# RG-LRU gates as 64x64 quadrants of the array, and an earlier split of w_ukv

## The chip, the cores and the metric

One core of a Trainium2 chip runs one launch of a whole transformer layer. The metric is the device time of that launch in microseconds (us); lower is better. TensorE (PE) multiplies, VectorE (DVE), ScalarE (ACT) and GpSimd (POOL) do the elementwise work, and SyncE (SP) issues all DMAs, in order. All data are float32 in memory; matmuls take either f32 operands or operands that were split into a high and a low part (fp32r).

## What is computed

A layer on 1024 latent and 256 context tokens (1280 columns together). The part that matters here is the RG-LRU mixer, 512 channels wide, and what follows it:

```
xr, gr, cq, ckv, kr = split(h @ w_in)             # gr, cq for latent tokens
xc = depthwise_conv(xr)                           # 4 taps
for d in (forward, backward):
    r = sigmoid(xc_by_head @ w_a[d] + b_a[d])     # 8 heads of 64 channels
    i = sigmoid(xc_by_head @ w_x[d] + b_x[d])
    log_a = -8 * r * softplus(-lam[d])
    h[d] = scan(a = exp(log_a), u = sqrt(-expm1(2*log_a)) * i * xc)   # context first, then latents
y_lru = (h[0] + h[1]) * gelu(gr)
keys, values = rms_norm(ckv) @ w_ukv ; queries = rms_norm(cq) @ w_uq  # MLA, 8 heads
x = x + gate1 * norm([y_lru, attention] @ w_out) ; x = x + gate2 * norm(conv_ffn(x))
```

The gates `r` and `i` multiply each head's 64 channels by a 64x64 matrix of that head.

## The kernel before

Channels lie on partitions, tokens on columns. The stage of the change is the loop over eight 128-channel blocks `m` of `w_in`: blocks 0 to 3 are `xr`, 4 to 7 `gr`. For each, `proj` makes the projection pf (L492, L494, L496: high and low parts, 128x512 pieces) in a PSUM buffer of 1536 columns; there are two such buffers (tag "big"), which projections and gates share. Between the projections `mod2_step` multiplies pages of `w_mod` for later stages (L424: 128x32 strips of the array, four 32-row outputs; L433 and L436 turn the result).

For m = 0 to 3, `conv` copies the projection (L532, L533 on ACT) and makes the convolution `xc[m]` on DVE (L537). The gates of block m come one projection later (`after = {1:0, 2:1, 3:2, 5:3}`): `gate` (L543) multiplies `xc[m]`, 128 channels, by a 128x128 block `wg` that holds two heads on its diagonal and zeros elsewhere, in three column pieces (`CH3`: 512, 512, 256), and ACT takes the sigmoid (L545). A block has four gates (two directions, r and i). `coefs` (L565, L566 on ACT; L567 on DVE) and `scans` follow: the square roots (L573 on ACT), then on DVE L578, L579, and two scans for each direction (L581, L582; L585, L587) and their sum (L591). `gated` multiplies the sum by the gelu of pf4 to pf7 (L552 on ACT, L553 on DVE).

For m = 5 the gates of block 3 run, then `tok_norm`, `ckv_t` (transposes L637, L641 and L642), then `scans(3)`. For m = 6 `w_ukv` is loaded and split by `prep_w` into `wkh` (L69 on ACT) and `wkl` (L76 on DVE). After the loop the cq transposes (L699, evacuated by L701 on ACT and L702 on DVE), five `values` blocks (L713 to L715, six matmuls each) and the keys (L728) follow, in four PSUM buffers; the cq transposes use two of them, so the third and fourth values wait for the two L702. POOL splits `w_uq` (L73, L76).

In this stage the order on each engine is made by the framework's scheduler when the program is built; engines then run in order and wait by semaphores. Pages of 128x1280 come from a pool R of 12, of 128x1024 from a pool L of 30 and W of 5; a load waits until its page is free.

Of the kernel before, what the change touches and what calls it, by code (L numbers as in the profile page):

```python
# [7 lines left out]
F32 = mybir.dt.float32  # L8
# [26 lines left out]
def hybrid_layer_kernel(ctx: ExitStack, tc: tile.TileContext, A, out):  # L35
    nc = tc.nc
    V, S, G, T = nc.vector, nc.scalar, nc.gpsimd, nc.tensor
# [10 lines left out]
    def L(dt=F32, shape=(128, 1024)):  # L48
        cnt[0] += 1
        return lp.tile(list(shape), dt, tag="L", name=f"l{cnt[0]}")  # L50

    def W(dt=F32, shape=(128, 1024)):
        cnt[0] += 1
        return wp.tile(list(shape), dt, tag="W", name=f"w{cnt[0]}")

    def R(dt=F32, shape=(128, 1280)):
        cnt[0] += 1
        return rp.tile(list(shape), dt, tag="R", name=f"r{cnt[0]}")
# [19 lines left out]
    def split(src, hi, lo_, eh, el):  # L78
        copy(eh, hi, src)
        return lo(el, lo_, src, hi)  # L80
# [10 lines left out]
    def P(name, i=0, n=None):  # L91
        o, w = _OFF[name]
        n = w - i if n is None else n
        return pk[:, o + i:o + i + n]
# [254 lines left out]
    for n in range(4, 16):  # L349
        b, kp = order[n]  # L350
# [122 lines left out]
    CH3 = ((0, 512), (512, 512), (1024, 256))  # L473

    def load_w(src):
        t = W()
        nc.sync.dma_start(out=t, in_=src)
        return t

    def prep_w(raw, eh, el):  # L480
        hi, lw = W(F32R), W(F32R)
        split(raw, hi, lw, eh, el)
        return hi, lw

    def proj(w, chunks, name):

        hi, lw = w
        po = ps1.tile([128, 1536], F32, tag="big", name=name, bufs=2)
        for k in range(8):
            wh, wl = hi[:, k * 128:(k + 1) * 128], lw[:, k * 128:(k + 1) * 128]  # L490
            for t0, n in chunks:
                T.matmul(po[:, t0:t0 + n], wh, h_rng(hhi, k, t0, n), start=(k == 0), stop=False)  # L492
            for t0, n in chunks:
                T.matmul(po[:, t0:t0 + n], wh, h_rng(hlo, k, t0, n), start=False, stop=False)  # L494
            for t0, n in chunks:
                T.matmul(po[:, t0:t0 + n], wl, h_rng(hhi, k, t0, n), start=False, stop=(k == 7))  # L496
        return po
# [20 lines left out]
    wg = {}  # L518

    def load_wg(m):  # L520
        wg[m] = L(F32, (128, 4, 128))
        nc.sync.dma_start(out=wg[m], in_=A["wg"][:, m * 512:(m + 1) * 512].rearrange("p (i n) -> p i n", i=4))

    SEG = ((0, SEQ), (SEQ, CTX))
    xc = {}

    def conv(m, po):

        xr = R()
        x = xc[m] = R()  # L530
        cw = [P("cw", m * 4 + k, 1) for k in range(4)]
        S.activation(xr, po[:, 0:NTOK], AF.Copy)  # L532
        S.activation(x, po[:, 0:NTOK], AF.Identity, scale=cw[2], bias=P("cb", m, 1))  # L533
        for o, n in SEG:
            for k, d in ((0, -2), (1, -1), (3, 1)):
                a, b = (o - d, o + n) if d < 0 else (o, o + n - d)
                V.scalar_tensor_tensor(out=x[:, a:b], in0=xr[:, a + d:b + d], scalar=cw[k], in1=x[:, a:b],  # L537
                                       op0=ALU.mult, op1=ALU.add)

    def gate(m, d, g):  # L540
        po = ps1.tile([128, 1536], F32, tag="big", name=f"pg{m}{d}{g}", bufs=2)
        for a, n in CH3:
            T.matmul(po[:, a:a + n], wg[m][:, d * 2 + g, :], xc[m][:, a:a + n], start=True, stop=True)  # L543
        r = R()
        S.activation(r, po[:, 0:NTOK], AF.Sigmoid, bias=P("bx" if g else "ba", d * 4 + m, 1))  # L545
        return r
# [3 lines left out]
    def gated(m, po):  # L550
        g = R()
        S.activation(g[:, :SEQ], po[:, :SEQ], AF.Gelu_apprx_tanh)  # L552
        V.tensor_tensor(ysum[m], ysum[m], g[:, :SEQ], ALU.mult)  # L553
# [4 lines left out]
    def coefs(m, ri):  # L558

        au = []  # L560
        for d in range(2):
            r, i = ri[d]
            c = slice(d * 4 + m, d * 4 + m + 1)
            a = R()
            S.activation(a, r, AF.Exp, scale=n8[:, c])  # L565
            S.activation(r, r, AF.Tanh, scale=p4[:, c])  # L566
            V.tensor_tensor(i, i, xc[m], ALU.mult)  # L567
            au.append((a, r, i))
        return au

    def scans(m, au):
        for a, b, h in au:
            S.activation(b, b, AF.Sqrt)  # L573
        hs = []
        for d in range(2):
            a, b, h = au[d]

            V.scalar_tensor_tensor(out=b, in0=a, scalar=1.0, in1=b, op0=ALU.add, op1=ALU.mult)  # L578
            V.tensor_tensor(h, b, h, ALU.mult)  # L579
            if d == 0:  # L580
                V.tensor_tensor_scan(out=h[:, SEQ:], data0=a[:, SEQ:], data1=h[:, SEQ:], initial=0.0, op0=ALU.mult, op1=ALU.add)  # L581
                V.tensor_tensor_scan(out=h[:, :SEQ], data0=a[:, :SEQ], data1=h[:, :SEQ], initial=h[:, NTOK - 1:NTOK],  # L582
                                     op0=ALU.mult, op1=ALU.add)
            else:
                V.tensor_tensor_scan(out=h[:, SEQ:][:, ::-1], data0=a[:, SEQ:][:, ::-1], data1=h[:, SEQ:][:, ::-1],  # L585
                                     initial=0.0, op0=ALU.mult, op1=ALU.add)
                V.tensor_tensor_scan(out=h[:, :SEQ][:, ::-1], data0=a[:, :SEQ][:, ::-1], data1=h[:, :SEQ][:, ::-1],  # L587
                                     initial=h[:, SEQ:SEQ + 1], op0=ALU.mult, op1=ALU.add)
            hs.append(h)
        ysum[m] = L()  # L590
        V.tensor_tensor(ysum[m], hs[0][:, :SEQ], hs[1][:, :SEQ], ALU.add)  # L591
# [60 lines left out]
    after = {1: 0, 2: 1, 3: 2, 5: 3}  # L652
# [5 lines left out]
    for n, m in enumerate(order):  # L658
        po = proj(ws, CH3 if m < 4 else CH3[:2], f"pf{m}")
        if n < 7:  # L660
            ws = prep_w(raw, "a", "v")
            if n < 6:
                raw = load_w(A["w_fm"][order[n + 2]])
        for s_ in STEPS2[n]:
            mod2_step(s_)
        if m < 4:
            load_wg(m)
            conv(m, po)
        else:
            gated(m - 4, po)  # L670
        if m in after:
            au = coefs(after[m], gates(after[m]))
            if m == 5:
                tok_norm()
                ckv_t()
            scans(after[m], au)
        if m == 6:
            raw = load_w(A["w_ukv"])
            wkh, wkl = prep_w(raw, "a", "v")
    pe_ctx.close()  # L680
    pe_ctx = ExitStack()
    ps2 = pe_ctx.enter_context(tc.tile_pool(name="ps2", bufs=4, space=PSUM, reuse_waits="tile"))
# [438 lines left out]
    for i in range(8):  # L1121
        po = out_tile(i)
# [296 lines left out]
    with tc.manual_schedule():  # L1419
# [13 lines left out]
        o, st = up_steps(*raw, V)  # L1433
# [47 lines left out]
        for j in range(1, NP):  # L1481
            if j + 1 < NP:
                if j == 1:
                    o, st = o2, {n: st2[n] for n in ("sums", "hi_u", "lo_u", "hi_g", "lo_g")}
                else:
                    o, st = up_steps(*raw)
# [7 lines left out]
            else:  # L1494

                o, nxt = None, None
# [258 lines left out]
```

## Time and profile before

| | |
|---|---|
| runs | 1312.43, 1312.20, 1311.76 us, median 1312.2 |
| profiled execution | 1312.39 us |
| its span, first to last instruction | 1310.6 us |
| mean granted PE clock | 0.99 |
| PE busy | 1272.8 us (97%) |
| DVE, ACT, POOL busy | 1011.1, 733.7, 387.3 us |
| gate matmuls (L543) | 96 instructions, 123.1 to 229.1 us |
| first attention matmul | 290.2 us |

The projection and gate stage is from about 90 to 253 us of the span. "Busy" PE means that a matmul is in it, not that all of the array works. The chain of waits goes back from the last instruction through whatever released each step; a row of the timeline merges equal instructions that follow each other and names, in brackets, how long the engine stood before them and what ended that.

### The profile page before, as it was taken

The page shows a single profiled execution, that of the slowest core. Times are in us where ns is not written, and L with a number is a line of the kernel's source. Part 1 is how long each engine was busy: PE and PEld are TensorE (multiplying, and loading weights), DVE is VectorE, ACT ScalarE, POOL GpSimd, SP SyncE. Part 2 cuts the span into 40 slices and gives each one's busy share as a digit, 9 for nine tenths or more (in the row PEclk, how much of TensorE's full clock was granted, in tenths as well). Part 3 has the DMA queues.
Part 4 walks back from the last instruction along what each step waited for, and adds up shares of the span by engine and source line. Part 5 has one row for each costly group of instructions (what it writes and reads, how often), then busy time and mean ns, then how long its engine had stood idle before and what let it go on. Part 6 is the DMA issues. An engine that isn't in the chain of part 4 may idle for free.

```text
span 1310.6 us, 17934 instructions
## 1 busy us (share of the span) xinstructions
PE 1272.8 (97%) x6490; PEld 1050.5 (80%) x6490; DVE 1011.1 (77%) x1665; ACT 733.7 (56%) x1374; POOL 387.3 (30%) x366
## 2 busy tenths in 40 slices
PE   5999999899999999999998999999999999999997
PEld 2796666687999999888877888888888888888886
DVE  3653577767898888856579898778777878897798
ACT  3543675557999999954365334433443344434581
POOL 2410000224666666743100433343244330000013
PEclk8999999999999999999999999999999999999999
DMA  9533234000000000242322222221222149205043
GB/s 372 198 123 125 93 121 145 25 1 2 2 1 2 2 1 17 96 163 97 144 85 91 100 71 90 97 86 65 92 97 81 65 143 354 97 1 177 2 145 128
DMA packets 41320, 124.21 MB, mean 95 GB/s; under 512 B 4600, under 2 KB 4880, under 8 KB 41232
## 3 DMA queue, kind: packets, MB, share of 16 engines
q1 hardware_dynamic: 41232, 123.07, 26.4%
q8 instruction: 51, 0.84, 0.3%
q14 instruction: 37, 0.30, 0.1%
HBM read 101.02 MB, written 22.03 MB: 94 GB/s over the span
## 4 chain that ended last, share of the span: by engine, by line
PE 83%; DVE 10%; ACT 4%; issue 2%; DMA 1%; SPq 0%; POOL 0%; DVEq 0%; ACTq 0%; POOLq 0%
PE b L1217 10%; PE b L1216 10%; PE b L1215 10%; PE t L914 5%; PE po L1063 4%; PE b L1391 4%; PE b L1393 4%; PE b L1392 4%; PE pg L543 3%; PE s L878 3%; PE o L938 3%; PE o L939 3%; PE s L879 3%; PE s L880 2%; DVE l L76 2%; PE po L1066 2%
## 5 line engine op out<-in xcount | busy, mean ns | idle before, releaser
L1217 PE MATMUL b<-l,f 128*128 128x512 f32 x620 | 242.7, 392 | 2.2 <-DVE f L76 2.2
L1215 PE MATMUL b<-l,f 128*128 128x512 f32 x620 | 242.7, 391 | 1.9 <-ACT f L1190 1.4
L1216 PE MATMUL b<-l,f 128*128 128x512 f32 x620 | 242.5, 391 | 0.9 <-DVE l L76 0.9
L1217 PEld LDWEIGHTS b<-l,f 128*128 128x128 f32 x620 | 117.1, 189 | 27.2 <-DVE f L76 3.0
L1215 PEld LDWEIGHTS b<-l,f 128*128 128x128 f32 x620 | 117.1, 189 | 27.0 <-ACT f L1190 1.9
L1216 PEld LDWEIGHTS b<-l,f 128*128 128x128 f32 x620 | 117.1, 189 | 26.1 <-DVE l L76 1.7
L1190 ACT ACTIVATE f<-w 128x1024 fp32r<-128x1024 f32 x21 | 22.3, 1060 | 202.0 <-POOL w L1187 193.7
L906 POOL TENSOR_SCALAR r<-r,c 128x512 f32<-128x512 f32 (+1 forms) x128 | 101.4, 805 | 97.7 <-DVE c L901 68.6
L883 DVE TENSOR_REDUCE c<-s 128x1 f32<-128x512 f32 (+1 forms) x192 | 108.7, 594 | 26.0 <-PE s L880 24.5
L76 DVE TENSOR_TENSOR f<-w,f 128x1024 fp32r<-128x1024 f32 (+1 forms) x90 | 98.3, 1094 | 33.9 <-ACT f L1190 32.9
L1274 DVE SCALAR_TENSOR_TENSOR l<-f,c,l 128x1023 f32<-128x1023 f32 x88 | 121.2, 1378 | 0.7
L894 ACT ACTIVATE r<-s,c 128x512 f32<-128x512 f32 (+1 forms) x192 | 117.7, 621 | 6.2 <-DVE c L901 4.7
L1184 POOL TENSOR_TENSOR w<-w 128x512 f32<-128x512 f32 x19 | 24.5, 1289 | 301.3 <-DVE f L76 301.3
L76 DVE TENSOR_TENSOR l<-t,l 128x512 fp32r<-128x512 f32 x128 | 81.5, 678 | 1.5 <-ACT l L69 1.3
L914 PE MATMUL t<-c,r 128*128 128x128 f32 x640 | 81.7, 273 | 0.9 <-DVE r L76 0.6
L69 ACT ACTIVATE l<-t 128x512 fp32r<-128x512 f32 x128 | 69.5, 595 | 8.6 <-PE t L914 7.8
L914 PEld LDWEIGHTS t<-c,r 128*128 128x128 f32 x640 | 71.3, 140 | 2.6 <-PE t L914 0.8
L1268 ACT ACTIVATE l<-f,c 128x1024 f32<-128x1024 f32 x44 | 54.5, 1238 | 31.7 <-DVE f L1255 31.2
L1614 POOL TENSOR_TENSOR f<-f,w 128x1024 f32<-128x1024 f32 (+1 forms) x5 | 11.8, 2372 | 202.7 <-ACT l L1580 202.7
L878 PE MATMUL s<-r,w 96*128 96x512 f32 (+1 forms) x192 | 69.5, 362 | 1.0 <-ACT r L894 0.7
L1063 PE MATMUL po<-l,r 128*128 128x512 f32 x256 | 69.3, 390 | 0.0
L938 PE MATMUL o<-l,r 128*128 128x256 f32 x256 | 69.0, 303 | 0.0
(355 smaller groups left out, 3195.3 us busy)
## 6 DMA issues: line engine op xcount, KB each, us to landing
w<-in_w_up SPq DMA_DIRECT2D x44, 512.0 KB
r<-in_w_mod SPq DMA_DIRECT2D x32, 512.0 KB
act<-l SPq DMA_DIRECT2D x22, 512.0 KB
l<-in_w_m SPq DMA_DIRECT2D x16, 512.0 KB
l<-act SPq DMA_DIRECT2D x27, 256.0 KB
l<-in_w_dn SPq DMA_DIRECT2D x27, 256.0 KB
w<-in_w_fm SPq DMA_DIRECT2D x8, 512.0 KB
w<-in_w_out SPq DMA_DIRECT2D x8, 512.0 KB
```

What stands on the lines that cost most here:

```text
L76: return (V if e == "v" else G).tensor_tensor(o, src, f(hi), ALU.subtract)
L878: T.matmul(ps[:, :n], qh[0:96, q], kh[0:96, a:a + n], start=True, stop=False)
L883: V.tensor_reduce(out=stat[:, i % 4, c:c + 1], in_=sc[i, c][:, :CK[c][1]], op=ALU.min, axis=AX.X)
L894: S.activation(pt_[i][:, a:a + n], sc.pop((i, c))[:, :n], AF.Exp, scale=-1.0, bias=st[:, 3:4], accum_out=st[:, 4 + c:5 + c])
L906: G.tensor_scalar(out=p[:, a:a + n], in0=p[:, a:a + n], scalar1=stat[:, i % 4, 7:8], scalar2=1.0, op0=ALU.mult, op1=ALU.mult)
L914: T.transpose(ps[:, c, :], pt_[i][:, (c0 + c) * 128:(c0 + c + 1) * 128], ident)
L938: T.matmul(OT[j], v, hi, start=(c == 0), stop=False)
L1063: T.matmul(po[:, n * 512:(n + 1) * 512], w, wo[k][0][:, n * 512:(n + 1) * 512], start=st, stop=en)
L1215: T.matmul(po, wh, bh, start=k == 0 and b == wb[0][1], stop=False)
L1216: T.matmul(po, wh, bl, start=False, stop=False)
L1217: T.matmul(po, wl, bh, start=False, stop=k == 3 and b == wb[-1][1])
L1274: V.scalar_tensor_tensor(out=x[:, a], in0=x0[:, b], scalar=P("fcw", j * 3 + k, 1), in1=x[:, a], op0=ALU.mult, op1=ALU.add)
```

## The change

The gates no longer use one 128x128 block. `load_wg` stores the two 64x64 matrices of each gate twice: `wg[m][:, 0]` as they are, and `wg[m][:, 1]` with the two halves of the partitions swapped, in four DMAs of 64x4x64 instead of one of 128x512. `conv` makes a copy `xcs[m]` of `xc[m]` with its two halves of partitions swapped, by two DMAs of 64x1280 from SBUF to SBUF. `gate` multiplies columns 512 to 1023 on the off-diagonal quadrants of the array (rows 64-127 to output 0-63 and rows 0-63 to output 64-127, from the swapped copies), and columns 0 to 511 and 1024 to 1279 on the diagonal quadrants. What follows the first matmul of a block's first gate in the program is kept behind it by `issue_after`. In the loop, `scans(3)` moves from m = 5 to m = 6, behind the split of `w_ukv`.

```diff
     def load_wg(m):
-        wg[m] = L(F32, (128, 4, 128))
-        nc.sync.dma_start(out=wg[m], in_=A["wg"][:, m * 512:(m + 1) * 512].rearrange("p (i n) -> p i n", i=4))
+
+        wg[m] = L(F32, (128, 2, 4, 64))
+        src = A["wg"][:, m * 512:(m + 1) * 512].rearrange("p (i n) -> p i n", i=4)
+        for x in range(2):
+            for b in (0, 64):
+                p = b ^ (64 * x)
+                nc.sync.dma_start(out=wg[m][p:p + 64, x], in_=src[b:b + 64, :, b:b + 64])
...
+        y = xcs[m] = R()
+        for p in (0, 64):
+            nc.sync.dma_start(out=y[64 - p:128 - p, :], in_=x[p:p + 64, :])
+
     def gate(m, d, g):
+
         po = ps1.tile([128, 1536], F32, tag="big", name=f"pg{m}{d}{g}", bufs=2)
-        for a, n in CH3:
-            T.matmul(po[:, a:a + n], wg[m][:, d * 2 + g, :], xc[m][:, a:a + n], start=True, stop=True)
+        first = None
+        for pieces in (((1, 512, 512), (0, 0, 512)), ((0, 1024, 256),)):
+            for x, a, n in pieces:
+                for o in (0, 64):
+                    h = o ^ (64 * x)
+                    i = T.matmul(po[o:o + 64, a:a + n], wg[m][h:h + 64, x, d * 2 + g, :], (xcs if x else xc)[m][h:h + 64, a:a + n],
+                                 start=True, stop=True, tile_position=(h, o))
+                    if first is None and (d, g) == (0, 0):
+                        first = i
+                        ctx_q.enter_context(tc.issue_after(first.ins))
+        ctx_q.close()
...
             if m == 5:
                 tok_norm()
                 ckv_t()
-            scans(after[m], au)
+                au3 = au
+            else:
+                scans(after[m], au)
         if m == 6:
             raw = load_w(A["w_ukv"])
             wkh, wkl = prep_w(raw, "a", "v")
+            scans(3, au3)
```

The order of the built programs shows it at three places. PE, the first gate of the first group (pm is the modulation, pg the gate), before:

```order
L424 MATMUL pm_952<-r_966,c_77 32x512 x2
L543 MATMUL pg_1109<-r_976,l_973 128x512
L433 MATMUL pm_1074<-c_84,r_1072 128x2 x4
L424 MATMUL pm_1084<-r_1064,c_77 32x512 x2
L424 MATMUL pm_1084<-r_1065,c_77 32x512 x2
L543 MATMUL pg_1109<-r_976,l_973 128x512
L543 MATMUL pg_1109<-r_976,l_973 128x256
```

And after, where the gate is line 558 (r_988 is the swapped copy, r_979 the convolution itself):

```order
L424 MATMUL pm_952<-r_966,c_77 32x512 x2
L558 MATMUL pg_1121<-r_988,l_973 64x512
L433 MATMUL pm_1080<-c_84,r_1078 128x2 x4
L424 MATMUL pm_1090<-r_1070,c_77 32x512 x2
L424 MATMUL pm_1090<-r_1071,c_77 32x512 x2
L558 MATMUL pg_1121<-r_988,l_973 64x512
L558 MATMUL pg_1121<-r_979,l_973 64x512 x2
L558 MATMUL pg_1121<-r_979,l_973 64x256 x2
```

One off-diagonal matmul stands alone ahead of L433, the other five together behind the modulation; the later gates have their six in a row. In the third group three L424 matmuls that stood behind the next projection now stand between the second and the third gate.

ACT, from the last square roots to the first cq evacuation, before (r_1657 is direction 0, r_1669 direction 1, w_1828 the high half of `w_ukv`, pf_1770 the projection pf6):

```order
L573 ACT_TABLE_LOAD
L573 ACTIVATE r_1657<-r_1657 128x1280
L573 ACTIVATE r_1669<-r_1669 128x1280
L552 ACT_TABLE_LOAD
L552 ACTIVATE r_1823<-pf_1770 128x1024
L69 ACTIVATE w_1828<-w_1826 128x1024
L552 ACTIVATE r_1881<-pf_1832 128x1024
```

After, with lines 593 for 573 and 572 for 552:

```order
L593 ACT_TABLE_LOAD
L593 ACTIVATE r_1720<-r_1720 128x1280
L69 ACTIVATE w_1888<-w_1886 128x1024
L572 ACT_TABLE_LOAD
L572 ACTIVATE r_1883<-pf_1830 128x1024
L593 ACT_TABLE_LOAD
L593 ACTIVATE r_1738<-r_1738 128x1280
L572 ACT_TABLE_LOAD
L572 ACTIVATE r_1953<-pf_1904 128x1024
```

The high half of `w_ukv` and the gelu of pf6 moved between the roots of the two directions, with two more table loads.

DVE at the same place, before (w_1829 is the low half of `w_ukv`):

```order
L578 SCALAR_TENSOR_TENSOR r_1657<-r_1677,r_1657 128x1280
L578 SCALAR_TENSOR_TENSOR r_1669<-r_1681,r_1669 128x1280
L579 TENSOR_TENSOR r_1663<-r_1657,r_1663 128x1280
L579 TENSOR_TENSOR r_1675<-r_1669,r_1675 128x1280
L581 SCALAR_TENSOR_TENSOR r_1663<-r_1677,r_1663 128x256
L585 SCALAR_TENSOR_TENSOR r_1675<-r_1681,r_1675 128x256
L582 SCALAR_TENSOR_TENSOR r_1663<-r_1677,r_1663 128x1024
L587 SCALAR_TENSOR_TENSOR r_1675<-r_1681,r_1675 128x1024
L553 TENSOR_TENSOR l_1492<-l_1492,r_1823 128x1024
L591 TENSOR_TENSOR l_1768<-r_1663,r_1675 128x1024
L76 TENSOR_TENSOR w_1829<-w_1826,w_1828 128x1024
L553 TENSOR_TENSOR l_1768<-l_1768,r_1881 128x1024
```

After (598 for 578, 599 for 579, 573 for 553, 601, 602, 605, 607 for the scans, 611 for the sum):

```order
L598 SCALAR_TENSOR_TENSOR r_1720<-r_1749,r_1720 128x1280
L76 TENSOR_TENSOR w_1889<-w_1886,w_1888 128x1024
L599 TENSOR_TENSOR r_1729<-r_1720,r_1729 128x1280
L573 TENSOR_TENSOR l_1552<-l_1552,r_1883 128x1024
L601 SCALAR_TENSOR_TENSOR r_1729<-r_1749,r_1729 128x256
L602 SCALAR_TENSOR_TENSOR r_1729<-r_1749,r_1729 128x1024
L598 SCALAR_TENSOR_TENSOR r_1738<-r_1753,r_1738 128x1280
L599 TENSOR_TENSOR r_1747<-r_1738,r_1747 128x1280
L605 SCALAR_TENSOR_TENSOR r_1747<-r_1753,r_1747 128x256
L607 SCALAR_TENSOR_TENSOR r_1747<-r_1753,r_1747 128x1024
L611 TENSOR_TENSOR l_1902<-r_1729,r_1747 128x1024
L573 TENSOR_TENSOR l_1902<-l_1902,r_1953 128x1024
```

The low half of `w_ukv` moved from the tenth place behind the first L578 to right behind it, and direction 0 now goes through its scans before direction 1 begins.

## Rows read from the trace of the kernel before

**Rows 1.** The page: PE's part 1, and part 4 by engine.
```profile
PE 1272.8 (97%) x6490; PEld 1050.5 (80%) x6490; DVE 1011.1 (77%) x1665; ACT 733.7 (56%) x1374; POOL 387.3 (30%) x366
PE 83%; DVE 10%; ACT 4%; issue 2%; DMA 1%; SPq 0%; POOL 0%; DVEq 0%; ACTq 0%; POOLq 0%
```

**Rows 2.** PE in order of time (start, length), modulation and first gate group.
```profile
105.10 2.78 PE L424 MATMUL pm<-r,c 128*32 128x512 f32 x24
...
123.08 1.12 PE L543 MATMUL pg<-r,l 128*128 128x512 f32 x2
124.04 0.95 PE L433 MATMUL pm<-c,r 128*128 128x2 f32 x8
...
131.58 1.06 PE L424 MATMUL pm<-r,c 128*32 128x512 f32 x6
132.57 4.56 PE L543 MATMUL pg<-r,l 128*128 128x512 f32 x12
136.79 0.93 PE L492 MATMUL pf<-l,w 128*128 128x512 f32 x3
```

**Rows 3.** PE in order of time, the modulation behind pf4.
```profile
203.20 2.59 PE L424 MATMUL pm<-r,c 128*32 128x512 f32 x14
```

**Rows 4.** ACT in order of time, the last gate group.
```profile
220.21 1.06 ACT L69 ACTIVATE w<-w 128x1024 fp32r<-128x1024 f32 x1
221.29 1.28 ACT L545 ACT_TABLE_LOAD   x1
222.58 1.33 ACT L545 ACTIVATE r<-pg,c 128x1280 f32<-128x1280 f32 x1
...
225.65 0.68 ACT L641 ACTIVATE l<-ck,c 128x512 fp32r<-128x512 f32 x1
...
229.16 1.33 ACT L545 ACTIVATE r<-pg,c 128x1280 f32<-128x1280 f32 x1 [0.82 <-PE pg L543]
```

**Rows 5.** The chain that ended last (start, length, what), 218 to 300 us.
```profile
239.18 1.28 ACT r L573
...
240.48 2.90 DVE r L578 x2
243.38 5.10 DVE r L579 x2
...
262.58 0.43 PE pb L715
...
266.33 0.23 PE pb L715
```

**Rows 6.** DVE and POOL in order of time, scans and w_uq.
```profile
205.60 2.88 DVE L579 TENSOR_TENSOR r<-r,r 128x1280 f32<-128x1280 f32 x2
...
260.23 2.46 DVE L702 SCALAR_TENSOR_TENSOR l<-pb,c,l 128x1024 fp32r<-128x1024 f32 x2
...
242.87 2.22 POOL L76 TENSOR_TENSOR l<-l,l 128x768 fp32r<-128x768 f32 x1 [9.61 <-PE pf L494]
```

**Rows 7.** PE in order of time, cq transposes, values and keys.
```profile
251.40 1.91 PE L699 MATMUL pb<-c,l 128*128 128x128 f32 x16
...
259.23 0.80 PE L714 MATMUL pb<-w,l 128*128 128x512 f32 x1 [5.68 <-DVE w L76]
...
268.44 0.39 PE L728 MATMUL pb<-l,w 128*128 128x512 f32 x1
```

**Rows 8.** Two stretches: each engine's busy us (count), then granted clock, DMA.
```profile
180.00:230.00 50.00, 50.00 (x204) 29.54 (x197) 41.21 (x53) 32.17 (x28) 0.00 (x0) 1.00 0.35 111
230.00:262.00 32.00, 26.32 (x120) 21.69 (x119) 24.16 (x17) 17.85 (x17) 6.98 (x4) 0.93 0.09 25
```

**Rows 9.** DVE, SP and POOL in order of time: first convolution, loads of w_uq.
```profile
108.16 4.86 DVE L537 SCALAR_TENSOR_TENSOR r<-r,c,r 128x1022 f32<-128x1022 f32 x6 [1.21 <-ACT r L533]
...
229.17 14.16 SPq L691 DMA_DIRECT2D l<-in_w_uq  x2
...
232.43 0.84 POOL L73 TENSOR_SCALAR l<-l 128x768 fp32r<-128x768 f32 x1 [59.97 <-DMA l<-in_w_uq]
```

More of the change, by code (lines that the diff above doesn't have):

```diff
@@ L520, in load_wg @@
     def load_wg(m):
-        wg[m] = L(F32, (128, 4, 128))
-        nc.sync.dma_start(out=wg[m], in_=A["wg"][:, m * 512:(m + 1) * 512].rearrange("p (i n) -> p i n", i=4))
+        wg[m] = L(F32, (128, 2, 4, 64))
[4 more added lines that the diff above has]
+                nc.sync.dma_start(out=wg[m][p:p + 64, x], in_=src[b:b + 64, :, b:b + 64])
     SEG = ((0, SEQ), (SEQ, CTX))
-    xc = {}
+    xc, xcs = {}, {}
+    ctx_q = ExitStack()
     def conv(m, po):
```

## The prediction

> **What bounds the kernel now.** I read the page first: PE is busy for 97% of the span and carries 83% of the chain that ended last, DVE 10% [rows 1]. Time is therefore won where PE does less, or where it stands. Then I read PE in order of time where the change works. In the gate groups PE goes from projection to gates to projection without standing: in the first group, 123.08 to 136.79 us, 12 gate instructions (two gates of 1280 columns; every f32 matmul is two instructions) take from 132.57 to 136.79, so 2.11 us a gate [rows 2]. From 229 us on it is another matter. The chain leaves PE with the last sigmoid and runs through ACT (Exp, Tanh, Sqrt) to DVE's scan chain, which starts at 240.48 [rows 4, 5]; PE meanwhile does two projections and the cq transposes, begins the values, and stands 5.68 us from 253.55 until DVE has made the low half of `w_ukv` [rows 7]. When it starts again its clock is at half: the same matmul takes 0.43 us at 262.58 and 0.23 at 266.33, and the mean granted clock of 230 to 262 is 0.93 [rows 5, 8]. From the keys (268.44) PE runs on into attention [rows 7], so what the keys gain, the end gains. The profiled execution took 1312.39 us (span 1310.6), the median of the three runs is 1312.2; I count against 1312.4.
>
> **A gate.** Now it is 512+512+256 columns of a 128x128 block with half of its entries zero. After: six 64x64 matmuls, two of 512 columns on the off-diagonal quadrants, two of 512 and two of 256 on the diagonal. The product of 512 columns costs 2.11x512/1280 = 0.84 us by itself, 256 cost 0.42. What the trace of before does not show is 64 rows of the array working beside the other 64. Bounds: one after another a gate would take 4x0.84+2x0.42 = 4.2 us; all four at once, the fullest quadrant has 768 columns, 0.6x2.11 = 1.27 us. The nearest row is the modulation (L424), 32-column strips of the array with different data: 24 instructions, three times four matmuls of 512 columns, take 2.78 us from 105.10 [rows 2], 2.72 of them ahead of the next projection; one by one they would take 12x0.84 = 10.1 us, so four do run at once, at 0.91 us a four. It has 128 rows and four strips, not two by two, but it is four independent f32 matmuls at once, which is the question; so I take 0.91x768/512 = 1.36 us a gate and gain 0.75.
>
> **The groups.** In every group the first off-diagonal matmul of the first gate stands alone, ahead of L433 or L436 (the order of PE), so that gate is 0.84+1.36 = 2.20 and loses 0.09. Three gates gain 2.25. The gates now change the array's shape against the 128x128 work around them, about two changes more a group; a lone gate matmul takes 0.96 from 123.08 to 124.04 where a run gives 0.84 [rows 2], so 0.12 a change, 0.2 a group. Net 1.95 a group, 5.9 for m = 0, 1, 2. PSUM has two buffers for gates, so gate n+2 waits for sigmoid n (1.33 us [rows 4]); with L424 work between the gates this does not bind there. For m = 2 the 14 L424 instructions of 203.20 (2.59 us) [rows 3] become 6 between the gates (1.06 like the six at 131.58 [rows 2]) and 8 where the 14 were (one and the same four, so as much): 0.5 gained. PE reaches the last group 6.4 us earlier.
>
> There ACT binds: the first sigmoid starts right behind its table load (221.29, 222.58 [rows 4]), which moves with PE's group, to 216.2. Now the four sigmoids wait for PE and end at 229.16+1.33 = 230.5. After, a gate (1.36) costs no more than a sigmoid, and they run back to back with the 0.66 us of L641 (225.65 [rows 4]) between: 4x1.33+0.66 = 6.0, end 222.2. **The scan chain starts 8.3 us earlier**, since from the last sigmoid to its start the same instructions follow (240.48 becomes 232.2).
>
> **The scan chain and the values.** Ahead of DVE's first L702 (the low half of cq, which frees the PSUM buffer of the third values block) the order shows the same twelve instructions in both programs: L76 only moves from behind the scans to between them. Their time also contains a collision: L579 takes 5.10 us for two where two took 2.88 at 205.60, while POOL splits `w_uq` (242.87) [rows 5, 6]. POOL is released by the eighth matmul of the last projection, which moves with everything else, so I leave that as it is; were it gone, 5.10-2.88 = 2.2 us would come back. So the first L702 ends 8.3 earlier, at 261.4-8.3 = 253.1 [rows 6].
> On ACT the split of `w_ukv` moves between the two L573 and costs two more table loads: d = 1 gets its root 4.7 us later (L69 1.06, L552 about as much, two loads of 1.28 [rows 4]). That hides as long as DVE is still in direction 0: ahead of that need it has one L578 and one L579 (half of 2.90 and of 5.10 [rows 5], 4.0 us) and L76, L553 and two scans besides. L69 and L552, and behind them DVE's L553, wait for the projection pf6; it starts behind the last gates and moves with them, as the scan chain does.
> PE: the last two projections end at 251.4 now [rows 7]; they move by the group's 6.4 and by what ACT leaves of the gates' gain in the last group, 1.2, to 243.8. Transposes take 1.9, two values of six matmuls (0.23 each at full clock [rows 5]) 2.7: 248.4. They no longer wait for L76. The third does wait, for L702 at 253.1: **4.7 us of standing, in place of 5.68**. Then three values are left, 4.1 us, at full clock. Now keys start (268.44) 7.0 us behind the first L702. If the clock stays up they start 4.1 behind it: 2.9 more. If it falls as before, the half pace costs 2.5 us (259.23 to 264.7) and only 0.4 remains. 4.7 is nearer to 5.68 than to nothing; I take the fall. **Gain 8.3+0.4 = 8.7 us; 1312.4-8.7 = 1303.7.** With the clock up 1301.2; with that and gates of 1.27 us 1300.3.
>
> **What else is issued.** Per m, two DMAs of 64x1280 (640 KB) that swap the halves of `xc`, and four for `wg` instead of one. They go into SP's queue, where the swap waits for the convolution and holds the `w_mod` and `w_fm` loads behind it. A load lands about 3.3 us after its issue (229.17 to 232.43) [rows 9]. The first convolution ends at 113.0 [rows 9], its gates start at 123.08, so 10 us cover twice that size; the other groups have more. Loads behind it are issued 6 us later than now, but are needed 10 or more later. The tightest is one `w_mod` page of m = 1, issued as the modulation ahead of the group starts and multiplied about 4.4 us later: 0 to 1 us. All this costs nothing while that cover holds. The new R pages take slots of the same 12; one wait is new, L532 of m = 2 behind L433, about 1 us on ACT, covered by PE's L424.
>
> **Rivals.**
> *The halves of a bank exclude each other (slower).* Both diagonal matmuls write PSUM columns 0-511, both others 512-1023: one bank, two halves of the partitions, from different halves of the rows. If such writes are taken in turn, only one diagonal and one off-diagonal matmul run together: 2x0.84+2x0.42 = 2.53 a gate, 0.42 over now, and the first gates 0.84+2.53 = 3.37, 1.26 over: 12x0.42+4x1.26 = 10.1, and 0.8 for the changes of shape, less 0.9 (the modulation and the values), so 1322.4; with nothing at all at once 16x2.1 more than now, about 1345. It decides from about 2.15 us a gate. Against it: L424's four strips write one bank at once; but they share their rows, these do not.
> The Trainium skill, "TensorEngine Tiling (Array Packing)", section "Gotcha 1: PSUM Pressure", says that different row tiles cannot access the same PSUM bank at the same time; by that rule the kernel lands on this rival. No run here shows it yet.
> *Only two at a time.* If halves of the columns run together but halves of the rows take turns, a gate is 2x0.84+0.42 = 2.1, as now; PE is where it was and only the values move: 0.4 to 2.9 less 0.8 for the changes of shape, 1310.3 to 1312.8. For it: no row shows row halves; against: nothing in L424 hints that rows matter.
> *A late load or DVE.* Quadrants work, but a late `w_mod` page, or DVE (41 of 50 us busy before 230 [rows 8]) reaching the R pages late, stops PE or the sigmoids for 1 to 2 us in two or three groups: gain 3 to 6, 1306 to 1309.5. For it: several sigmoids now start within 0.5 us of the scan that frees their page.
>
> **Numbers.** Forecast (1299.5 to 1305.5, with the two clocks and the bounds of a gate) 0.70; late load 0.10; two at a time 0.12; banks or nothing at once 0.08. The first two hold 0.8, so the range is 1299.5 to 1309.5. A measurement tells 0.2%, 2.6 us. Faster by more: 0.70+0.10+0.01 = 0.81; within: 0.11; slower: 0.08.
>
> **What would show it.** Two gates in a row in 2.7 us and not 4.2; next projections starting 2, 4 and 6 us earlier; the last four sigmoids back to back; L578 near 232; PE waiting for L702, no longer for L76; half clock there or not. It is wrong if a gate takes 2.1 us or more, if PE waits for the swapped copies, or if DVE waits in direction 1 for ACT's late root.

## The result and the profile after

| | before | after |
|---|---|---|
| runs, median | 1312.32 us (1311.76 to 1313.38, 4 runs) | 1305.22 us (1304.05 to 1307.54, 4 runs) |
| ratio, 95% interval | | 0.9947 (0.9930 to 0.9964) |
| profiled execution, its span | 1312.39, 1310.6 | 1307.54, 1305.7 |
| PE busy | 1272.8 us | 1265.6 us |
| last sigmoid starts | 229.16 [rows 4] | 223.56, the second of the two in the row from 222.33 |
| DVE's last scans start | 240.48 [rows 5] | 234.88 |
| PE stands ahead of the values | 5.68 [rows 7] | 5.66 |
| keys start | 268.44 [rows 7] | 264.05 |
| first attention matmul | 290.19 | 285.76 |

7.1 us were gained where 8.7 were forecast. The profiled execution of after happens to be the slowest of the four, with 4.9 us of gain, and 4.4 of these are there at the first attention matmul. The traces start their clocks at different points: the 24 instructions of L424 ahead of all gates begin at 105.10 in before [rows 2] and at 104.32 in after. So I compare the *stage* from there to the first attention matmul: 185.1 us before, 181.4 in this execution. From the first attention matmul on, every trace of this study takes 1018.8 to 1020.4 us, so what the stage gains, the end gains, to within 1.6 us. The four longest of these tails (1020.0 us and more, in before, after, rows_ahead and evac) go with the lowest granted clock near 710 us (0.83 or 0.84 over 20 us there, 1.00 in after_again), a place that no kernel of this study changes: of the 3.6 us between the profiled executions of after and after_again, about 1 lies there.

PE in order of time, first gate group (start, length, count):

```profile
122.30 1.07 PE L558 MATMUL pg<-r,l 64*64 64x512 f32 x2
123.30 1.05 PE L433 MATMUL pm<-c,r 128*128 128x2 f32 x8
...
125.27 1.51 PE L558 MATMUL pg<-r,l 64*64 64x512 f32 x10
126.72 1.90 PE L424 MATMUL pm<-r,c 128*32 128x512 f32 x10
128.55 1.52 PE L558 MATMUL pg<-r,l 64*64 64x512 f32 x12
...
130.99 2.81 PE L558 MATMUL pg<-r,l 64*64 64x512 f32 x24
133.94 0.85 PE L492 MATMUL pf<-l,w 128*128 128x512 f32 x3
```

Two gates (24 instructions) take 2.81 us where two took 4.56 [rows 2], so four quadrants do run at once. The group from its first gate matmul to the next projection is 11.64 us, 13.71 before: 2.07 gained, and in the second group 2.05 (10.79 for 12.84).

The gain does not arrive whole. PE in order of time at the modulation behind pf4, which answers to [rows 3]:

```profile
197.02 1.05 PE L424 MATMUL pm<-r,c 128*32 128x512 f32 x4
199.87 1.05 PE L424 MATMUL pm<-r,c 128*32 128x512 f32 x4 [1.80 <-DMA r<-in_w_mod]
200.85 0.80 PE L492 MATMUL pf<-l,w 128*128 128x512 f32 x2
...
202.30 1.05 PE L496 MATMUL pf<-l,w 128*128 128x512 f32 x2
...
205.30 0.62 PE L492 MATMUL pf<-l,w 128*128 128x512 f32 x2
```

PE waits 1.80 us for a page of `w_mod`, and then works at half clock (a granted clock of 0.5): a row of two projection matmuls takes 1.05 where it takes 0.62 three microseconds later. The last group starts at 215.42, 3.3 us before its old time (218.68), or 2.5 with the traces laid on each other, that is less the 0.78 us between their two starts of L424, and not 6.4. What held the page, in the chain of waits (start, length, what):

```profile
190.36 0.42 DVE r L444
190.80 3.63 DMA gt<-r
194.51 5.31 DMA r<-in_w_mod
```

SP's waits from 170 to 210 us (total, times, longest), and SP in order of time:

```profile
...
SPq L445 <- DVE r L444: 6.6, 1, 6.6
...
SPq L548 <- DVE r L543: 2.3, 1, 2.3
...
SPq L411 <- DMA gt<-r: 1.6, 1, 1.6
```

```profile
185.79 0.23 SPq L445 DMA_DIRECT2D gt<-r  x1
...
189.52 1.16 SPq L548 DMA_DIRECT2D r<-r  x2
190.80 0.77 SPq L445 DMA_DIRECT2D gt<-r  x1
191.67 10.10 SPq L411 DMA_DIRECT2D r<-in_w_mod  x6
```

SP's queue stands 6.6 us for a first small row that DVE makes in the modulation (L444, written to DRAM by L445 at 185.79) and 2.3 for DVE's convolution of block 3 (the swap, L548, at 189.52). Right behind the swap it writes a second such row (190.80) and issues the first page (191.67). The second page (L411, at 194.51 inside that row of six) waits 1.6 until the second write has landed; why this load depends on that write no run here shows. DVE's side moved less than PE did.

ACT, DVE and POOL in order of time, last gates to cq, which answer to [rows 4 to 6]:

```profile
219.32 2.54 ACT L565 ACTIVATE r<-pg,c 128x1280 f32<-128x1280 f32 x2
...
222.33 2.57 ACT L565 ACTIVATE r<-pg,c 128x1280 f32<-128x1280 f32 x2
...
234.88 1.49 DVE L598 SCALAR_TENSOR_TENSOR r<-r,r 128x1280 f32<-128x1280 f32 x1 [1.80 <-ACT r L593]
...
239.43 2.87 DVE L573 TENSOR_TENSOR l<-l,r 128x1024 f32<-128x1024 f32 x1
...
242.93 2.35 DVE L602 TENSOR_TENSOR_SCAN r<-r,r 128x1024 f32<-128x1024 f32 x1
245.20 2.05 DVE L598 SCALAR_TENSOR_TENSOR r<-r,r 128x1280 f32<-128x1280 f32 x1
247.29 2.99 DVE L599 TENSOR_TENSOR r<-r,r 128x1280 f32<-128x1280 f32 x1
...
255.90 2.47 DVE L725 SCALAR_TENSOR_TENSOR l<-pb,c,l 128x1024 fp32r<-128x1024 f32 x2
...
238.40 2.82 POOL L76 TENSOR_TENSOR l<-l,l 128x768 fp32r<-128x768 f32 x1 [8.61 <-PE pf L494]
243.19 2.73 POOL L73 TENSOR_SCALAR l<-l 128x768 fp32r<-128x768 f32 x1 [1.97 <-DMA l<-in_w_uq]
246.00 2.93 POOL L76 TENSOR_TENSOR l<-l,l 128x768 fp32r<-128x768 f32 x1
```

The four sigmoids now run back to back. But from the first L598 to the end of the first L725 DVE takes 22.3 us (234.88 to 257.1), where before took 21.0 (240.48 to 261.5 [rows 5, 6]): every DVE row with two operands from SBUF that starts under a POOL instruction is stretched past the end of that instruction (L573, the second L598, the second L599); the first L599 (238.02), which starts before POOL does, is not.

PE there, which answers to [rows 7]:

```profile
257.23 0.79 PE L736 MATMUL pb<-w,l 128*128 128x512 f32 x1 [5.66 <-DVE l L725]
...
262.52 0.54 PE L736 MATMUL pb<-w,l 128*128 128x512 f32 x1
...
264.05 0.39 PE L751 MATMUL pb<-l,w 128*128 128x512 f32 x1
```

As forecast, PE now stands for L725 (the line that is L702 in the kernel before), about as long as it stood for L76, and its clock falls again: until 262.52 a matmul starts every 0.43 us, from there every 0.23.

### The profile page after: what moved, and what is told of

It reads as the page before. It is cut to its first block, busy times and chain, and to the rows that moved or that the text cites. A ratio compares the mean times of both kernels' runs of the same rounds, so it can differ in the third digit from the quotient of the medians.

```text
span 1305.7 us, 18162 instructions
## 1 busy us (share of the span) xinstructions
PE 1265.6 (97%) x6586; PEld 1042.3 (80%) x6586; DVE 1012.0 (78%) x1665; ACT 735.5 (56%) x1376; POOL 388.9 (30%) x366
## 4 chain that ended last, share of the span: by engine, by line
PE 81%; DVE 10%; ACT 4%; DMA 3%; issue 2%; SPq 0%; DVEq 0%; POOL 0%; ACTq 0%; POOLq 0%
PE b L1240 10%; PE b L1238 10%; PE b L1239 10%; PE t L937 5%; PE po L1086 4%; PE b L1415 4%; PE b L1416 4%; PE b L1414 4%; PE o L961 3%; PE o L962 3%; PE s L901 3%; PE s L902 3%; PE s L903 3%; DVE l L76 2%; PE po L1089 2%; PE pf L492 2%
## 5 line engine op out<-in xcount | busy, mean ns | idle before, releaser
L1213 ACT ACTIVATE f<-w 128x1024 fp32r<-128x1024 f32 x21 | 22.3, 1060 | 201.9 <-POOL w L1210 193.6
L76 DVE TENSOR_TENSOR f<-w,f 128x1024 fp32r<-128x1024 f32 (+1 forms) x90 | 98.4, 1095 | 34.1 <-ACT f L1213 33.1
L76 DVE TENSOR_TENSOR l<-t,l 128x512 fp32r<-128x512 f32 x128 | 81.5, 679 | 1.5 <-ACT l L69 1.3
```

Of the source, the lines that this page charges most:

```text
L76: return (V if e == "v" else G).tensor_tensor(o, src, f(hi), ALU.subtract)
```

## The experiments

"Stage" is the stretch defined above, from each kernel's own profiled execution; the other columns are medians and the ratio to the runs of before on the same chip.

| kernel | median us | ratio, 95% interval | stage us |
|---|---|---|---|
| before | 1311.3 to 1312.3 | 1 | 185.1 |
| after | 1305.22 | 0.9930 to 0.9964 | 181.4 |
| after_again | 1305.02 | 0.9937 to 0.9962 | 179.0 |
| gates_only | 1305.07 | 0.9937 to 0.9962 | 178.5 |
| split_only | 1311.66 | 0.9994 to 1.0012 | 186.0 |
| copies_only | 1311.17 | 0.9986 to 1.0003 | 185.4 |
| rows_ahead | 1303.85 | 0.9934 to 0.9959 | 178.6 |
| rows_swap | 1301.48 | 0.9906 to 0.9933 | 175.9 |
| pool_late | 1299.84 | 0.9895 to 0.9924 | 173.5 |
| split_evac | 1302.73 | 0.9914 to 0.9941 | 177.1 |
| evac | 1296.27 | 0.9861 to 0.9894 | 171.1 |
| evac_rows | 1294.69 | 0.9853 to 0.9883 | 169.4 |
| evac_rows_swap | 1293.19 | 0.9843 to 0.9870 | 167.3 |
| pairs | 1314.16 (one run) | | 188.5 |

### The changed kernel once more (after_again; no edit)

> The changed kernel once more, beside its own variants. The theory: what is missing from the forecast gain (8.7 forecast, 7.1 measured, 4.9 in the profiled execution) went in two places of the stage before the attention: a page of w_mod that PE waits for at 199.87 us (1.80 us of standing, then about 1.6 us of half clock in the next projection), and DVE's last scans, which take 22.2 us from the first L598 to the first L725 against 20.9 before. If the wait is there in each execution but the clock falls only in some, executions come in two kinds, near 1304 and near 1307 us, and a profile of the first kind shows the wait with 0.23 us matmuls behind it. The rival is that the spread has nothing to do with that page: then profiles of quick and slow executions show the same stretch of 197 to 214 us.

1305.02 us, 1303.89 to 1305.98; the profiled execution is the quickest of the five. PE in order of time at the same place:

```profile
196.84 1.05 PE L424 MATMUL pm<-r,c 128*32 128x512 f32 x4
199.66 1.05 PE L424 MATMUL pm<-r,c 128*32 128x512 f32 x4 [1.77 <-DMA r<-in_w_mod]
200.65 0.73 PE L492 MATMUL pf<-l,w 128*128 128x512 f32 x2
```

The stretch of 196 to 207 us (length, busy us of PE, its loads, DVE, ACT and POOL with counts, granted clock, DMA share, GB/s), in after:

```profile
196.00:207.00 11.00, 9.20 (x33) 5.77 (x32) 10.82 (x8) 4.55 (x5) 0.00 (x0) 0.84 0.66 234
```

and here:

```profile
196.00:207.00 11.00, 9.23 (x41) 5.98 (x40) 10.97 (x8) 4.40 (x4) 0.00 (x0) 1.00 0.68 228
```

The wait is the same, 1.77 for 1.80; the granted clock fell behind it in one execution (0.84 over these 11 us) and not in the other (1.00). That is 1.6 us: from the end of the wait to the last group's modulation 13.70 us in after (199.87 to 213.57) and 12.09 here (199.66 to 211.75). So the wait without the fall, which the theory asked for, is there, and the rival falls: the two profiles do not show the same stretch. The two kinds of execution, near 1304 and near 1307 us, are not: of the nine executions of this kernel one took 1307.54, two 1303.89 and 1304.05, and six lie between, at 1304.87 to 1305.98. Three more traces of this study keep the same wait, gates_only (1.84 us), pool_late (1.80) and evac (1.83), and in all three the granted clock is 1.00 over 196 to 207 us: the fall behind this wait was seen in one trace of five. The stage is 2.4 us shorter than in after: 1.6 of it here, the rest behind 253 us.

### One part of the change each (gates_only, split_only)

```
 gates_only: the changed kernel, m == 5
             ckv_t()
-                au3 = au
-            else:
-                scans(after[m], au)
+            scans(after[m], au)
...
-            scans(3, au3)
 split_only: the kernel before, the same move the other way
```

> The quadrant gates with scans(3) left in its old place. The theory of the prediction: the move of the scans is worth 0.4 us, because PE stands about as long before the values either way; so this kernel lies within 1 us of the changed one, with PE waiting for L76 (the low half of w_ukv) and not for L725. The rival: the move of the scans carries a good part of the gain (2.9 us where the clock stays up), and this kernel is 2 to 3 us slower than the changed one.

> The kernel before with only the move of scans(3) behind the split of w_ukv. The theory: PE goes through the first two values and then stands for L702 in place of L76; 0.4 us faster than before, 1311.9 us, within the error. The rival that the move is worth 2.9 us gives 1309.4; the rival that ACT's two extra table loads reach DVE in direction 1 makes it 1 to 3 us slower than before.

gates_only (1305.07) is the changed kernel (1305.02) to 0.1 us, split_only is the kernel before (interval of the ratio around 1; a gain of 0.4 us would lie inside it). PE in order of time, gates_only, then split_only:

```profile
253.31 0.80 PE L734 MATMUL pb<-w,l 128*128 128x512 f32 x1 [4.55 <-DVE w L76]
```

```profile
262.68 0.80 PE L716 MATMUL pb<-w,l 128*128 128x512 f32 x1 [6.13 <-DVE l L705]
```

Both stand, one for L76, the other for the first low half of cq (L705 there). The move changes only for whom PE stands; the gates are the whole gain. The rivals fall: that the move carries 2 to 3 us of it, and that ACT's two more table loads cost 1 to 3.

### The late page (copies_only, rows_ahead, rows_swap)

```
 copies_only (kernel before, conv):
+        y = R()
+        for p in (0, 64):
+            nc.sync.dma_start(out=y[64 - p:128 - p, :], in_=x[p:p + 64, :])
 rows_ahead (changed kernel, mod2_step):
-    rw, gr = (mr[0:2, 512 + 256 * x:768 + 256 * x] for x in range(2))
     for h in range(2):
+        rw, gr = (mr[0:2, a_:a_ + 256] for a_ in ((512, 768), (1024, 0))[h])
 rows_swap (rows_ahead): the swap of block 3 leaves conv(3)
     for s_ in STEPS2[n]:
         mod2_step(s_)
+    if m == 4:
+        swap(3)
```

> The kernel before with the two swap DMAs per block and their R page, which nothing reads; the gates are the old ones. The prediction's step that the copies cost nothing while their cover holds says: within 0.5 us of before. The theory that the swap of block 3, which waits for DVE's convolution at the head of SP's queue, holds the w_mod loads of pf4 says: PE waits there 0.5 to 2 us more than the 0.3 to 0.5 us it waits now, and the kernel is 0.5 to 2 us slower than before; with the clock falling behind that wait, up to 3.5.

> The changed kernel, but the four small rows of step L442 go to four different places of their page, so that the write of the gate row (L445) no longer waits for a second round of loads; the second w_mod page of pf4's modulation, which is queued behind that write and behind its landing, is issued some 5 us earlier. The theory: the wait at 199.87 us is gone, PE reaches the last gate group about 3 us earlier than in the profiled execution of the changed kernel, and the time falls to 1302 to 1304 us, with the executions closer together. The rival (DVE's scan chain binds whatever PE does): the wait is gone and the time stays at 1304 to 1306.

> rows_ahead with the swap of block 3 issued behind pf4's modulation loads in place of ahead of them. The theory: what is left of the wait in rows_ahead (0.55 and 0.46 us at 198.2 and 199.7) is gone, PE goes into pf5 1.0 us earlier, and the last sigmoids, DVE's chain and the end follow: 1302.5 to 1303.5 us. The rival (the loads are late for another reason, such as their pages): the waits stay and the time is that of rows_ahead.

copies_only: 1311.17, not slower. Of what ended PE's idle time at the rows of L424 from 195 to 215 us (us, times) its trace has for that page

```profile
  DMA r<-in_w_mod: 0.2, 1
```

where before has 0.5. The copies by themselves cost nothing, and the theory that the swap holds the loads falls for the old gates, with which PE comes later. The median of rows_ahead is 1.2 us below after_again, but its five runs (1303.38 to 1305.86) lie among those of after_again (1303.89 to 1305.98) and no closer together, so a gain is not shown. The wait is shorter (0.55 and 0.46) and not gone as expected: there the first pages wait for the swap of block 3 in place of the row. In rows_swap it is gone, and PE does the eight instructions in one go. PE in order of time, rows_ahead, then rows_swap:

```profile
198.22 1.05 PE L424 MATMUL pm<-r,c 128*32 128x512 f32 x4 [0.55 <-DMA r<-in_w_mod]
199.73 1.05 PE L424 MATMUL pm<-r,c 128*32 128x512 f32 x4 [0.46 <-DMA r<-in_w_mod]
```

```profile
197.86 1.06 PE L424 MATMUL pm<-r,c 128*32 128x512 f32 x8
198.86 0.73 PE L492 MATMUL pf<-l,w 128*128 128x512 f32 x2
```

SP in order of time in rows_swap, where the pages go ahead of the swap (L553 there; after's rows stand above):

```profile
187.78 3.48 SPq L411 DMA_DIRECT2D r<-in_w_mod  x4
193.74 1.16 SPq L553 DMA_DIRECT2D r<-r  x2
```

The page costs more than its wait. Each of the two pages fills two of the four strips of the array, and the four instructions of one page take 1.05 us alone, as long as the eight of both together (1.06). When PE stands between them it loses the 1.80 and another 1.0, 2.8 in all: from 197.02 to 200.85 (3.83) in after against 197.86 to 198.86 (1.00) here. rows_swap was expected at 1302.5 to 1303.5, with the waits alone counted, and came to 1301.48; the lost pairing is the rest. With the page in time the change is worth 9.2 us of stage (185.1 to 175.9), and rows_swap's own median is 10.4 below that of its before.

### POOL's share in DVE's chain (pool_late)

```
     for k in range(2): ...
+        if k == 0:
+            tick = G.tensor_scalar(out=kt1[:, 0, 0:1], in0=ysum[3][:, 0:1], ...)
+            tick_q.enter_context(tc.issue_after(tick.ins))
         split(raw, h_, l_, "g", "g")
```

> The changed kernel with POOL's split of w_uq held back until DVE has made the last y_lru (one POOL instruction of one column that reads it stands ahead of the split). The theory: DVE's last scans are stretched by POOL's work, L573 2.87 against 1.23, the second L598 2.06 against 1.49, the second L599 2.99 against 1.49, 3.7 us together; without it the first L725 ends 3.7 us earlier, PE stands about 2 us in place of 5.66, and the keys start 3.7 to 5 us earlier: 1300 to 1301.5 us. The rival: the stretch is not POOL's doing, or goes over to L611, L573 and L725: no change. A second rival: w_uq comes late for the queries (about 6.3 us of POOL work from 251): PE waits there and 1 to 2 us are lost again.

DVE and PE in order of time:

```profile
238.91 1.22 DVE L573 TENSOR_TENSOR l<-l,r 128x1024 f32<-128x1024 f32 x1
...
243.03 1.47 DVE L598 SCALAR_TENSOR_TENSOR r<-r,r 128x1280 f32<-128x1280 f32 x1
244.54 1.49 DVE L599 TENSOR_TENSOR r<-r,r 128x1280 f32<-128x1280 f32 x1
...
251.65 2.47 DVE L730 SCALAR_TENSOR_TENSOR l<-pb,c,l 128x1024 fp32r<-128x1024 f32 x2
...
252.98 0.50 PE L741 MATMUL pb<-w,l 128*128 128x512 f32 x1 [1.92 <-DVE l L730]
```

1299.84, a little below the 1300 to 1301.5 expected: the three rows take 1.22, 1.47 and 1.49, the chain to the first low half of cq 18.6 us in place of 22.3, PE stands 1.92 and its clock stays up (the next matmuls follow at 0.23). 5.2 us were gained on the changed kernel for 3.7 taken out of DVE: the rest is the clock that no longer falls. The late page is still there (1.80 at 200.91). Both rivals fall: the stretch was POOL's, and from the keys to the first attention matmul PE takes 21.7 us (257.24 to 278.90) as in after_again (261.52 to 283.19), so the later `w_uq` costs nothing.

### Taking DVE's chain out of PE's way (evac, split_evac, evac_rows, evac_rows_swap)

```
 evac (changed kernel), cq:
-        S.activation(h_, pt, AF.Copy, scale=P("gq", k, 1))
-        V.scalar_tensor_tensor(out=l_, in0=pt, ...)
+        S.activation(raw, pt, AF.Copy, scale=P("gq", k, 1))
...
+    for raw in cqr:
...
+        split(raw, h_, l_, "a", "v")
 values:
-        copy("a" if p % 2 else "v", v, pv)
+        copy("a", v, pv)
 split_evac: the same on split_only; evac_rows, evac_rows_swap: evac with the edits of rows_ahead, of rows_swap
```

> The changed kernel, but ACT takes the cq transposes out of PSUM as they are (two copies of about 1.05 us), the two parts are split from that copy, and ACT takes out all values blocks, so that no PSUM buffer before the keys waits for DVE's scan chain. The theory that the chain to L725 is what sets the start of the keys: PE's standing of 5.66 us ahead of the third value is gone, its clock stays up there (5.3 or 4.0 us at half pace, 2 to 2.6 lost), and the keys start 6 to 8 us earlier; the end follows by 4 to 7 us, 1298 to 1301, less what the queries wait for the low part of cq, which DVE makes behind the scans. The rival: DVE is late for something right behind (the queries, the copies of the keys), and the gain is taken back there: 1304 to 1305.

> The kernel before with the scans behind the split of w_ukv and the PSUM evacuations of evac, so with the old gates. It prices the gates where no wait for DVE stands between them and the keys. PE's standing of 6.1 us ahead of the third value (split_only) should be gone: 1304 to 1306 us. Then the gates are worth the distance to evac (1296.3): by the forecast's 6.4 to 7.6 us of PE time less 1.8 for the late page, 5 to 8 us. If evac's gain came only with the new gates, this kernel stays at 1309 to 1312.

> evac with the rows of step L442 in four places as in rows_ahead. If the wait for the w_mod page and the one for L725 are both on the path once the second is gone, the gains add: 1.2 us below evac (what rows_ahead measured against the changed kernel), or more, since PE's arrival now counts and not DVE's. If DVE's chain still sets the queries, no more than evac.

> evac_rows with the swap of block 3 behind the modulation loads, as in rows_swap. PE's arrival counts in full here, so the 0.8 and 0.2 us of waiting left in evac_rows come off the end: 1293.5 to 1294 us. If it stays at 1294.7, the loads are late for another reason.

In all four PE goes from the cq transposes to the keys without standing. In evac the keys start at 254.09 and the first wait behind them is for the rotation of the keys (L808):

```profile
254.09 0.39 PE L754 MATMUL pb<-l,w 128*128 128x512 f32 x1
...
261.78 0.41 PE L777 MATMUL pb<-l,l 128*128 128x384 f32 x1 [0.52 <-DVE r L808]
```

evac is 8.7 us faster than the changed kernel, more than the 4 to 7 expected, and the queries do not wait for the low half of cq: up to the first attention matmul PE has no other wait than these 0.52 us and one of 0.34. split_evac, with the old gates, gains 9.2 on before, 1.3 beyond its expectation. So the edit, which takes out the standing and the half clock behind it, is worth about 9 us with either kind of gates. With it, the new gates are worth 6.5 us (1302.73 to 1296.27), and 9.5 where the page is in time (1293.19). evac_rows took 1.6 off evac and evac_rows_swap 1.5 more; I had written 1.2 and about 1. evac_rows_swap is the fastest kernel of this study, 1.4% below before.

### Two quadrants in place of four (pairs)

```
 (kernel before, gate)
-            T.matmul(po[:, a:a + n], wg[m][:, d * 2 + g, :], xc[m][:, a:a + n], start=True, stop=True)
+            for o in (0, 64):
+                T.matmul(po[o:o + 64, a:a + n], wg[m][o:o + 64, d * 2 + g, o:o + 64], xc[m][o:o + 64, a:a + n],
+                         start=True, stop=True, tile_position=(o, o))
```

> The kernel before with its gates as 64x64 blocks on the diagonal quadrants alone: 512, 512 and 256 columns, two matmuls at once, half of the rows each, both into the same columns of PSUM. If the two halves run together, a gate takes 2.1 us as with one 128x128 block, and two in a row 4.3 to 4.6 us; the time is that of the kernel before. If halves of the rows that write one bank take turns, a gate takes 4.2 us, and 16 of them make the kernel some 30 us slower.

```profile
133.32 4.51 PE L544 MATMUL pg<-r,l 64*64 64x512 f32 x24
```

Two gates take 4.51 us, as with 128x128 blocks (4.56 [rows 2]): the two row halves work at the same time on the same columns of PSUM, each on its own half of the partitions. There is one run of this kernel, 2.2 us above the median of before, so its time says little. Its first gates have a lone matmul ahead of L433 as after has, and this one stands without its partner: the first gate takes 1.00 and 2.29 us (122.93 and 125.91), where before takes 0.96 and 1.48.

## Why the prediction was right, and where it was not

The time, 1305.2, lies in the range and 1.5 us above the forecast. That it stayed so near is in part luck: a late page (2.8 us) and a longer DVE chain (1.2) that the sum had at nothing were partly made up by groups and sigmoids that gained more than I said (0.9) and a shorter half clock (0.4), and against the runs of before made beside after_again the gain is 6.2 us and not 7.1. Three of the nine executions (1305.57, 1305.98, 1307.54) lie above the forecast's own band, which ends at 1305.5, and inside the wider range. Of the steps:

- **A gate, 1.36 us, a group 1.95:** right, 2.07 and 2.05 a group; two gates in a row take 2.81 us. The first gate takes 1.00 and 1.45 us, 2.45 in place of 2.20, and gains nothing (2.44 before); the other three gain 2.2 together, as I said (2.25). That four independent f32 matmuls of L424 run at once was the right row to take the rate from. The rival of the PSUM banks falls twice, in after and in pairs. The Trainium skill, "TensorEngine Tiling (Array Packing)", section "Gotcha 1: PSUM Pressure", says that different row tiles cannot access one PSUM bank at the same time; here two row tiles that write different partitions of one bank do, at no cost that the 4.51 and 2.81 us show, and the measurement decides.
- **PE reaches the last group 6.4 us earlier:** this step failed: 2.5 with both traces laid on each other at the 24 L424 (3.26-0.78), 4.2 in after_again (5.08-0.92). The gates did their part: the projection behind the third group starts 5.4 us earlier (192.00 and 185.87, less 0.78), the shorter modulation behind pf4 adds 1.5 (203.20 to 205.72 before, 2.52; 1.00 in rows_swap), so 6.9; the page takes 2.8 of it, which leaves 4.1, and in after the clock 1.6 more. The term at fault is "Loads behind it are issued 6 us later than now, but are needed 10 or more later". Here the second page is issued at 194.51 and PE is free for it at 198.07, 3.6 us later, and it takes 5.31 us to land, where I had counted 3.3 for a load. I had looked for the tightest load among the first groups and never at pf4's, where no gate stands ahead. The cover of these pages was used up before the change: in the trace of before, the rows of L424 from 195 to 210 us list, among what ended PE's idle time (us, times),

```profile
  DMA r<-in_w_mod: 0.5, 1
```

  That load moves with its own queue, not with PE. By the traces' own times PE came 6.2 us earlier (203.20 to 197.02) and the issue 4.2 (198.71 to 194.51). The rival of the late load had the right mechanism; its place was named only as "a late page", its price (1 to 2 us) missed the lost pairing of the strips and the clock: 2.8, and 1.6 more in one of two traces of this kernel. rows_swap takes that term out, and its stage gains 9.2 us for the 8.7; its scan chain starts 9.2 earlier (laid on before) for the 8.3, DVE's chain gives 0.7 of that back, and the half clock, shorter than in before, returns 0.7.
- **Four sigmoids back to back:** right, 219.32 to 224.9. The scan chain starts 5.6 us earlier (4.8 laid on each other, 6.4 in after_again) for 8.3; what is missing is the page and the clock behind it.
- **The chain to the first L725 as long as before:** 22.3 for 21.0. "I leave that as it is" for POOL's collision was the mistake: L76 and the two directions stand in another order, so other instructions meet POOL. pool_late shows 3.7 us of collision where I had 2.2 in L579 [rows 5, 6]. How each row ends could have been worked out. L573 starts at 239.43 under POOL's L76, which ends at 241.22, and ends 1.08 behind that (alone it takes 1.22); L598 starts under L73, which ends at 245.92, and ends 1.33 behind it (alone 1.47); L599 starts under the next L76, which ends at 248.93, and ends 1.35 behind it (alone 1.49). The Trainium skill, "SBUF — State Buffer", section "SBUF: two separate sides", says so: a DVE instruction with two operands from SBUF and a GpSimd one that reads SBUF exclude each other for a whole instruction, and the later waits. The trace agrees, the other way too: L73 takes 2.73 under the scan L602 and 0.83 elsewhere.
- **What PE stands for, and the clock:** right. L725 in place of L76, 5.66 us for 4.7, half clock again; the move worth 0.4 measured as nothing (gates_only, split_only). I put what changes there down as a remainder of 0.4 us; evac and split_evac show that 8.7 and 9.2 us were to be had there, with the old gates as well.
- **The copies:** nothing, right for their own cost (copies_only), wrong for their place in SP's queue once PE came early (rows_ahead, rows_swap).

Added up from after_again, whose clock did not fall at the page: 8.7, less 1.9 by which its scan chain starts later than forecast (6.4 us earlier for 8.3: the page's 2.8, less 0.9 that groups and sigmoids gained beyond the forecast), less 1.2 in DVE's chain, and 0.4 back since PE worked at half clock for 4 us there and not 5.5: 6.0, and its stage shows 6.1. The terms are read from that trace, so the sum says where the gain went and is no second test. The medians show 6.2 and 7.1 of gain with the two sets of before. What the seven executions of this kernel without a trace did at the page stays open.

## What to carry to other kernels

When a faster stage moves an engine ahead, list every wait that the engine already has in that stage, however short: such a wait is a chain of its own, and it need not move with the engine (here 4.2 us for 6.2). Price a late operand with what it breaks up (matmuls that would have run side by side), and order changes on DVE with what POOL does at that moment, instruction by instruction. Where an engine stands for a PSUM buffer that a long chain on another engine has to empty, let an idle engine empty it and do the arithmetic from SBUF: here this gave more than the change itself.

## What the runs showed of the hardware

- Four 64x64 quadrants of the array work at once on f32, each with its own weights and data; a gate of six matmuls takes 1.4 us (half of 2.81) where two at a time take 2.25 (half of 4.51).
- Four 128x32 strip instructions that fill two of the four strips take 1.05 us, eight that fill all four 1.06 (after, rows_swap).
- The three DVE rows with two SBUF operands that start under a POOL instruction in after end 1.08, 1.33 and 1.35 us behind the end of that instruction, each 0.14 less than its own time: they take 1.22, 1.47 and 1.49 alone (pool_late).
- The granted clock after one and the same standing of 1.8 us: 0.84 over 11 us in after, 1.00 in after_again, gates_only, pool_late and evac. In the 5.66 us of standing ahead of the third value it fell in both after and after_again while PE still stood, 1.2 and 2.8 us before PE went on, and PE then worked at half clock for 5.3 and for 4.0 us.
- Standing of 1.92 us at 252.98 in pool_late left the clock up.
